# Loading the first weight piece in halves between the quarters of x, with the first squares taken bank by bank

## The chip, the core and the metric

The kernel runs on one core of a Trainium2 chip. The metric is the device time of one execution in microseconds; the number compared is the median of several runs. Five engines work side by side, each with its own queue in order: TensorE (PE, matrix products and transposes; its weight loads are PEld), VectorE (DVE), ScalarE (ACT), GpSimd (POOL) and SyncE (SP), which here only issues DMA transfers from HBM.

## What is computed

Two layers of an encoder on 256 tokens of width 1024, all in float32. What matters here is how the first layer begins:

```
def rms_norm(x, g, eps=1e-6):
    return x * rsqrt(mean(x * x, axis=-1) + eps) * g
def swiglu(x, w_in, w_out):
    gate, up = split(x @ w_in, 2, axis=-1)
    return (silu(gate) * up) @ w_out
for i in range(2):
    h = x + 0.5 * swiglu(rms_norm(x, norm_ffn1[i]), w_ffn1_in[i], w_ffn1_out[i])
    ...   # windowed attention beside a convolution, gated; a second swiglu; a gated input embedding
```

`w_ffn1_in` has 1024 rows and 2 x 2816 columns: 22 blocks of 128 gate columns and 22 of up columns.

## The kernel before, in words

**Products in three passes.** float32 operands are each split in a high and a low part (`w_hi`, `w_lo`, and `x0h`, `x0l` for the first x). A product is the sum of three: hi by hi, hi by the low part of x, low weight by hi. One block of 128 weight columns takes 8 row blocks (k = 0 to 7) times 3 matmuls, 24 in all. A gate block and an up block make a pair, `gate_up(j)`, with 48 matmuls and one PSUM tile `ps_gu`; there are 22 pairs. `by_pass` (line 349) runs the three passes one after the other over k, so that it can begin while `w_lo` is not there yet; `mm3` (line 338) goes through k once with three matmuls each and so needs both parts at once. Line 345 in the profile is mm3's matmul, line 354 by_pass's. Only pair 0 uses by_pass in the kernel before.

**Weights.** `Weights` (`ws`) keeps a list of units (one HBM transfer each into one of 5 `raw` buffers, line 83) and of specs (a 128-column piece, split by `prep_upto` into `w_hi` by a ScalarE cast, line 109, and `w_lo` by a VectorE subtraction, line 110; 7 buffers of each). `get()` hands out the next spec, first running hooks that are due, and then prepares specs up to 6 ahead; loading runs 3 units ahead of the unit that is being split. Specs 0 to 3 (pairs 0 and 1) have a unit of 512 KB each; after that a unit has 1 MB and serves two specs: units 4 and 5 serve specs 4 to 7 (pairs 2 and 3), units 6 and 7 the specs 8 to 11, and so on. The transfers go through SP's queue in order. x itself (`x_ld`, 1 MB, four transfers of a quarter, line 198) takes one of the 5 `raw` buffers too, so unit 4 can be loaded only when x has been transposed.

**The start.** PE first runs warm-up products (`work`, line 191; each shows as two records) on a constant, then transposes the parameter rows (`ps_par`, line 222) and x, 128 columns (one k) at a time with two transposes each (line 528), each k into a PSUM bank of its own; `WAIT[k]` puts extra `work` ahead of a k, and `BRIDGE` ahead of the first product. ScalarE makes `x0h` from PSUM with the norm's gain (line 534), VectorE `x0l` (line 535). Then spec 0 is split in two halves, and the first product begins. In between, x is copied to SBUF (`x32`, line 516), and its squares are formed: ScalarE squares one k (lines 446 and 448), GpSimd adds it to `sq_acc` (line 449). Here the order on ScalarE and VectorE is the program's (`manual_schedule`); later a scheduler with its own time model sets it, and `ws.behind` keeps the splits of later specs behind the last square.

**The norm.** The gate_up products use x without the norm's factor; it is multiplied in when `ps_gu` is read (`evac`, line 625). The factor comes from `Stat`: `divide` splits `sq_acc` into `sum_h` and `sum_l` (lines 503 and 504), `done` sums over the partitions by two matmuls (`ps_stat`, line 466), then come a square root on ScalarE (`sd`, line 414, with a table load) and a reciprocal on VectorE (line 416). `done` is due with spec 5. Until then no `ps_gu` can be read and freed. PSUM holds four one-bank tiles (`mm_tile`) and two two-bank tiles (`at_tile`); in the kernel before every `ps_gu` of the first stage is an `mm_tile`, and so is `ps_stat`.

**Late loads.** `hooks` call `late_loads` ahead of pair 1: 14 small transfers on SP's queue (line 562, parameters for later). `late_params` (hook ahead of pair 5) transposes the rows on PE (`ps_par`, line 222 again).

## Time and profile before

| what | value |
|---|---|
| runs | 1088.31, 1088.95 and 1089.26 us; median 1088.95 |
| profiled execution | 1086.72 us, of which the span of the program's instructions is 1084.9 |
| PE busy | 1076.1 us of the span |
| first product's first matmul | 9.65 us after the start |
| pair 1 begins | 15.32 us |
| pair 2 begins | 20.76 us |
| pair 3 begins | 29.54 us |
| last gate_up product ends | 133.65 us |

How to read it: times in a timeline count from the span's start. A PE instruction is listed with its whole duration (275 ns for a 128x256 matmul), but matmuls overlap and follow one another every 0.113 us, so the busy share of PE says only where it was not waiting. A note such as [0.83 <-DVE w_lo L110] says that the engine sat idle for 0.83 us until that instruction released it.

### The profile page before, as it was taken

The numbers are of one execution on the slowest core, as the hardware profiler recorded it, in microseconds if no ns is written. First come the engines' busy times: TensorE is split into PE (matmuls) and PEld (weight loads), VectorE is DVE, ScalarE is ACT, GpSimd is POOL, SyncE is SP. The second block draws the span as 40 slices with busy tenths as digits, with TensorE's granted clock in tenths as the row PEclk, the third lists the DMA queues.
The fourth block names the chain that finished last, engine by engine and source line by source line (L and its number), as shares of the span: only waits on it lengthen the run. The fifth ranks groups of instructions, "written<-read, shape, count | busy, mean of one in ns | idle before, by whom it ended". The sixth has DMA issues, their size and how long they took to land.

```text
span 1084.9 us, 22084 instructions
## 1 busy us (share of the span) xinstructions
PE 1076.1 (99%) x9180; PEld 1058.9 (98%) x9180; DVE 821.4 (76%) x1228; ACT 627.4 (58%) x1055; POOL 85.0 (8%) x156
## 2 busy tenths in 40 slices
PE   9999999999999999999999999999999999999998
PEld 8999999999899999999999999999998999999998
DVE  6777666799988777656887776669999987776664
ACT  7655445676766555445675554548776665554453
POOL 3100001120002000001110000112100100000110
PEclk9999999999999999999999999999999999999999
DMA  9786546556066656546555554666533666564531
GB/s 312 243 282 209 179 167 223 173 191 187 7 237 235 216 173 210 179 166 231 184 198 200 190 188 147 210 233 195 156 117 134 211 209 208 182 196 147 203 117 40
DMA packets 195612, 202.95 MB, mean 187 GB/s; under 512 B 3936, under 2 KB 188848, under 8 KB 195512
## 3 DMA queue, kind: packets, MB, share of 16 engines
q1 hardware_dynamic: 195480, 201.53, 56.0%
q8 instruction: 72, 1.18, 0.4%
q14 instruction: 28, 0.23, 0.1%
q10 hardware_dynamic: 32, 0.01, 0.0%
HBM read 200.46 MB, written 1.06 MB: 186 GB/s over the span
## 4 chain that ended last, share of the span: by engine, by line
PE 83%; DVE 9%; ACT 4%; issue 2%; POOL 1%; DMA 1%; SPq 0%; DVEq 0%; ACTq 0%; POOLq 0%
PE ps_gu L345 43%; PE ps_fo L345 22%; PE ps_wo L345 4%; DVE y L682 4%; PE ps_pe L345 4%; DVE w_lo L110 3%; PE ps_ao L959 3%; PE ps_c L345 2%; PE ps_co L1063 2%; ACT w_hi L109 1%; PE ps_pp L345 1%; DVE s L848 1%; PE ps_g L345 1%; ACT s L856 1%; DMA raw<-in_w_ffn_in_dram 1%
## 5 line engine op out<-in xcount | busy, mean ns | idle before, releaser
L110 DVE TENSOR_TENSOR w_lo<-raw,w_hi 128x1024 fp32r<-128x1024 f32 (+2 forms) x377 | 450.8, 1202 | 195.7 <-ACT w_hi L109 195.5
L109 ACT CAST w_hi<-raw 128x1024 fp32r<-128x1024 f32 (+2 forms) x377 | 387.7, 1034 | 352.1 <-PE ps_gu L345 189.7
L345 PE MATMUL ps_fo<-h_hi,w_hi 128*128 128x256 f32 x704 | 193.0, 275 | 0.0
L345 PE MATMUL ps_fo<-h_lo,w_hi 128*128 128x256 f32 x704 | 193.0, 275 | 0.0
L345 PE MATMUL ps_fo<-h_hi,w_lo 128*128 128x256 f32 x704 | 193.0, 275 | 0.0
L345 PEld LDWEIGHTS ps_fo<-h_hi,w_hi 128*128 128x128 f32 x704 | 131.9, 188 | 0.0
L345 PEld LDWEIGHTS ps_fo<-h_lo,w_hi 128*128 128x128 f32 x704 | 131.9, 188 | 0.0
L345 PEld LDWEIGHTS ps_fo<-h_hi,w_lo 128*128 128x128 f32 x704 | 131.9, 188 | 0.0
L449 POOL TENSOR_TENSOR sq_acc<-sq_acc,sq 128x256 f32<-128x256 f32 x56 | 52.9, 944 | 810.4 <-ACT sq L448 810.0
L682 DVE SCALAR_TENSOR_TENSOR y<-cpad,cw,y 128x256 f32<-128x256 f32 x240 | 100.7, 476 | 0.2
L345 PE MATMUL ps_gu<-xf0h,w_hi 128*128 128x256 f32 x352 | 96.8, 275 | 0.0
L345 PE MATMUL ps_gu<-xf1h,w_hi 128*128 128x256 f32 x352 | 96.8, 275 | 0.0
L345 PE MATMUL ps_gu<-xf0h,w_lo 128*128 128x256 f32 x352 | 96.7, 275 | 0.0
L345 PE MATMUL ps_gu<-xf1h,w_lo 128*128 128x256 f32 x352 | 96.7, 275 | 0.0
L345 PE MATMUL ps_gu<-xf0l,w_hi 128*128 128x256 f32 x352 | 96.7, 275 | 0.0
L345 PE MATMUL ps_gu<-xf1l,w_hi 128*128 128x256 f32 x352 | 96.7, 275 | 0.0
L345 PE MATMUL ps_gu<-xn0h,w_lo 128*128 128x256 f32 x352 | 96.6, 275 | 0.0
L345 PE MATMUL ps_gu<-xn0l,w_hi 128*128 128x256 f32 x352 | 96.6, 275 | 0.0
L345 PE MATMUL ps_gu<-xn0h,w_hi 128*128 128x256 f32 x352 | 96.5, 275 | 0.0
L345 PE MATMUL ps_gu<-x0h,w_hi 128*128 128x256 f32 x336 | 92.8, 276 | 1.7 <-ACT sd L414 1.7
L345 PE MATMUL ps_gu<-x0h,w_lo 128*128 128x256 f32 x336 | 92.6, 276 | 0.8 <-DVE w_lo L110 0.8
L345 PE MATMUL ps_gu<-x0l,w_hi 128*128 128x256 f32 x336 | 92.5, 275 | 0.0
(266 smaller groups left out, 2691.8 us busy)
## 6 DMA issues: line engine op xcount, KB each, us to landing
raw<-in_w_ffn_in_dram SPq DMA_DIRECT2D x86, 1024.0 KB
raw<-in_w_in_dram SPq DMA_DIRECT2D x30, 1024.0 KB
raw<-in_w_ffn_out_dram SPq DMA_DIRECT2D x32, 896.0 KB
raw<-in_w_ffn_out_dram SPq DMA_DIRECT2D x16, 1024.0 KB
raw<-in_w_o_dram SPq DMA_DIRECT2D x8, 1024.0 KB
raw<-in_w_pe_gate_dram SPq DMA_DIRECT2D x8, 1024.0 KB
raw<-in_w_attn_out_dram SPq DMA_DIRECT2D x8, 512.0 KB
raw<-in_w_conv_out_dram SPq DMA_DIRECT2D x4, 1024.0 KB
```

The costliest lines, as they stand in the source:

```text
L109: nc.scalar.copy(out=hv[:, at, d0 : d0 + w], in_=src),
L110: nc.vector.tensor_tensor(out=lv[:, at, d0 : d0 + w], in0=src, in1=hv[:, at, d0 : d0 + w].bitcast(F32), op=ALU.subtract,),
L345: mm = nc.tensor.matmul(ps, wa[:, k0 + k, cols], xa[:, kx, :], start=a, stop=b)
L449: nc.gpsimd.tensor_tensor(out=self.acc, in0=self.acc, in1=sq, op=ALU.add)
L682: last_tap[0] = nc.vector.scalar_tensor_tensor(out=y[:, i, :], in0=src, scalar=w, in1=y[:, i, :], op0=ALU.mult, op1=ALU.add)
L848: nc.vector.tensor_tensor_reduce(out=s[:, c, :], in0=ps[:, c, :], in1=bias[:, v * GROUP + c, off : off + T], scale=1.0, scalar=sink[:, hd ...
L856: nc.scalar.activation(out=s[:, c, :], in_=s[:, c, :], func=AF.Exp, bias=nm[:, c : c + 1], accum_out=den[:, c : c + 1],)
L959: nc.tensor.matmul(ps[:, c * T : (c + 1) * T], w[:, k, c * P : (c + 1) * P], x[:, k, :], start=k == 0, stop=k == KC - 1,)
L1063: mm = nc.tensor.matmul(ps[:, c, :], wa[:, k, c * P : (c + 1) * P], ya[:, k, :], start=(i, k) == (0, 0), stop=(i, k) == (2, KC - 1),)
```

## The change

Four things are changed, all in the first layer's start.

1. **Transfers.** Only two quarters of x are issued first. Unit 0 (and unit 1) are loaded as two halves of 4 k each, and the other two quarters of x are issued between and behind unit 0's halves: x0, x1, half a of unit 0, x2, half b, x3, unit 1 in halves, units 2 and 3.
2. **The first product.** PE transposes k = 0 to 3, does the hi-by-hi pass for them, transposes 4 and 5, does what has become possible, transposes 6 and 7, and does the rest. On ScalarE and VectorE the splits of x and of the weight's halves follow the same order. k and k + 4 share a PSUM bank. WARM goes from 7 to 6, WAIT from (0,0,1,0,2,0,2,0) to (0,0,2,0,0,0,0,0), BRIDGE from 4 to 2.
3. **Squares and copies.** Each bank (two k) is squared and copied to `x32` by one instruction of 512 columns. The first two squares go to a PSUM tile, the other two to SBUF; VectorE adds them, and GpSimd adds nothing. The splits of specs 2 to 5 are placed by hand between them, and `divide` runs in this order too, ahead of spec 5's split.
4. **Pairs.** Pairs 0, 1 and 2 go pass by pass, the others by mm3. Pair 0's `ps_gu` is an `at_tile`. `late_loads` moves from the hook ahead of pair 1 to that ahead of pair 2.

```
-WARM, WAIT, BRIDGE = 7, (0, 0, 1, 0, 2, 0, 2, 0), 4
+WARM, WAIT, BRIDGE = 6, (0, 0, 2, 0, 0, 0, 0, 0), 2
...
             for place, src in sources:
                 self.nc.sync.dma_start(place(v), src)
+                if self.next_load == 0:
+                    self.between.pop(0)()
...
+    ws.between = [lambda i=i: load_x(i) for i in (2, 3)]
...
-                        u = cols_unit(w_in, KD, c0 + c * P, P)
+                        u = cols_unit(w_in, KD, c0 + c * P, P, () if c else (KC,))
...
+    first_ps = at_tile("ps_gu").rearrange("p (c t) -> p c t", c=2)[:, :, :T]
...
+        splits = []
+        ws.cuts = (KC,)
+        ws.prep_upto(0, splits)
+        w_first = ws.ready[0]
+        turn_x(0, 1)
+        split_x(0, 1)
+        turn_x(2, 3)
+        split_x(2, 3)
+        work(BRIDGE, first_ps[:, 0, :])
+        for call in splits[:2]:
+            call()
+        steps((0, 0, 4))
+        turn_x(4, 5)
+        split_x(4, 5)
+        for call in splits[2:]:
+            call()
+        steps((1, 0, 4), (2, 0, 4), (0, 4, 6))
+        turn_x(6, 7)
+        split_x(6, 7)
+        steps((1, 4, 6), (2, 4, 6), (0, 6, 8), (1, 6, 8), (2, 6, 8))
         ws.prep_upto(1)
...
+        def keep_x(b):
+            nc.vector.tensor_copy(out=x32[:, b::KC, :], in_=banks[b])
+        ps_sq = at_tile("ps_sq").rearrange("p (b c t) -> p b c t", b=2, c=2)
+        sums = [tmp.tile([P, 2, T], F32, name="sq2", tag="gu") for _ in range(2)]
+        def square(b):
+            nc.scalar.activation(out=ps_sq[:, b] if b < 2 else sums[b - 2], in_=banks[b], func=AF.Square)
+        def plus(out, in0, in1):
+            nc.vector.tensor_tensor(out=out, in0=in0, in1=in1, op=ALU.add)
+        for b in range(2):
+            square(b)
+            keep_x(b)
+            ws.prep_upto(2 + b)
+        for b in range(2, KC):
+            square(b)
+            plus(sums[b - 2], sums[b - 2], ps_sq[:, b - 2])
+        plus(sums[0], sums[0], sums[1])
+        stat.acc = tmp.tile([P, T], F32, name="sq_acc", bufs=1)
+        plus(stat.acc, sums[0][:, 0, :], sums[0][:, 1, :])
+        ws.prep_upto(4)
+        divided, _ = stat.divide()
+        for b in range(2, KC):
+            keep_x(b)
+        ws.prep_upto(5)
+    ws.rest = LOOK
+    ws.get()
+    ws.rest = 0
+    ws.behind = (divided.ins,)
...
-            ps, products = pair("ps_gu", x_in, j == 0, early=x_in is x_first)
+            ps, products = pair("ps_gu", x_in, j == 0, early=x_in is x_first and j < 3)
...
-            hooks = {1: lambda: late_loads(hp), 5: late_params, 6: lambda: late_tables(hp), 8: late_write, 12: late_bias} if l == 0 else {}
+            hooks = {2: lambda: late_loads(hp), 5: late_params, 6: lambda: late_tables(hp), 8: late_write, 12: late_bias} if l == 0 else {}
```

`turn_x(k)` runs WAIT[k] and the two transposes of k, `split_x(k)` makes `x0h` and `x0l` of k, `splits` holds the cast and the subtraction of each half of spec 0, and `steps((pass, from, to), ...)` issues the matmuls of the first product for those k, pinned in this order on PE as every by_pass matmul now is.

## The prediction

> **What bounds the kernel now.** I read the page first, for the engine that is busy, then a table of stretches of the start, then the chain of waits through it.

> ```profile
> PE 1076.1 (99%) x9180; PEld 1058.9 (98%) x9180; DVE 821.4 (76%) x1228; ACT 627.4 (58%) x1055; POOL 85.0 (8%) x156
> ```
> ```profile
> 20.76:27.60 6.84, 6.01 (x52) 5.80 (x50) 6.84 (x7) 6.80 (x8) 0.11 (x1) 1.00 0.85 300
> 27.60:29.54 1.94, 0.21 (x2) 0.01 (x2) 1.94 (x3) 1.91 (x4) 0.00 (x0) 1.00 0.02 4
> 46.56:133.65 87.09, 87.09 (x771) 87.09 (x770) 64.34 (x88) 45.87 (x71) 0.00 (x0) 1.00 0.65 217
> ```

> PE (first busy column of the stretches) is the bound: it is idle for some 9 us of a span of 1084.9. So an edit is worth the idle PE time that it removes, and the rest of the kernel, which follows PE, moves along. In steady work 771 records take 87.09 us, 0.113 us a matmul, 2.72 for a block of 24 and 5.44 for a pair. The change touches nothing behind the first pairs, so only the start can pay: the first two stretches, in which PE stood for 0.83 and 1.73 us while DVE and ACT (third and fourth column) were full. The PE rows and the chain say on what:

> ```profile
> 4.62 1.11 PE L528 MATMUL ps_xt<-ident,x_ld 128*128 128x128 f32 x4
> 5.53 0.44 PE L191 MATMUL ps_xt<-ones_d 128*128 128x128 f32 x2
> 5.81 0.60 PE L528 MATMUL ps_xt<-ident,x_ld 128*128 128x128 f32 x4
> ```
> ```profile
> 9.65 1.26 PE L354 MATMUL ps_gu<-x0h,w_hi 128*128 128x256 f32 x8 [0.43 <-ACT w_hi L109]
> ...
> 15.32 0.28 PE L345 MATMUL ps_gu<-x0h,w_hi 128*128 128x256 f32 x1
> ...
> 22.00 0.39 PE L345 MATMUL ps_gu<-x0h,w_lo 128*128 128x256 f32 x1 [0.83 <-DVE w_lo L110]
> ...
> 29.54 0.39 PE L345 MATMUL ps_gu<-x0h,w_hi 128*128 128x256 f32 x1 [1.73 <-ACT sd L414]
> ```
> ```profile
> 15.97 1.62 POOL sq_acc L449
> ...
> 19.25 0.42 ACT sq L448
> 19.67 0.95 ACT w_hi L109
> ...
> 29.01 0.48 ACT sd L414
> ...
> 40.75 0.07 PE ps_par L222
> ```

> The squares pass to and fro between ACT and GpSimd until 19.67; only then comes spec 4's cast, too late for pair 2, which began at 20.76 and stood for 0.83 us until 22.00 for its `w_lo`. The same sum makes the root late: pair 3 waits until `sd` is done at 29.49, since four one-bank PSUM tiles hold pairs 0 to 2 and `ps_stat`.

> **The change part by part.** Prices come from these groups of the start on ACT and on DVE (busy time, then mean ns of one), the order from the ACT rows, the transfers from three stretches:

> ```profile
> L109 ACT CAST w_hi<-raw 128x1024 fp32r<-128x1024 f32 x3 | 3.2, 1053 | 0.4 <-DMA raw<-in_w_ffn_in_dram 0.4
> L448 ACT ACTIVATE sq<-x 128x256 f32<-128x256 f32 x3 | 1.1, 418 | 0.0
> L516 ACT COPY x<-ps_xt 128x256 f32<-128x256 f32 x2 | 0.6, 372 | 0.0
> L109 ACT CAST w_hi<-raw 128x512 fp32r<-128x512 f32 x1 | 0.6, 616 | 0.0
> ```
> ```profile
> L110 DVE TENSOR_TENSOR w_lo<-raw,w_hi 128x1024 fp32r<-128x1024 f32 x12 | 14.6, 1257 | 4.2 <-ACT w_hi L109 4.2
> L416 DVE RECIPROCAL r_x<-sd 128x256 f32<-128x256 f32 x1 | 1.7, 1740 | 0.0
> L516 DVE COPY x<-ps_xt 128x256 f32<-128x256 f32 x4 | 1.4, 416 | 0.0
> L110 DVE TENSOR_TENSOR w_lo<-raw,w_hi 128x512 fp32r<-128x512 f32 x2 | 1.3, 684 | 0.0
> L625 DVE TENSOR_TENSOR gu<-ps_gu,r_x 128x512 f32<-128x512 f32 x2 | 1.3, 673 | 0.0
> ```
> ```profile
> 5.42 3.42 ACT L534 ACTIVATE x0h<-ps_xt,par 128x256 fp32r<-128x256 f32 x8 [0.51 <-PE ps_xt L528]
> 8.98 1.14 ACT L109 CAST w_hi<-raw 128x512 fp32r<-128x512 f32 x2
> 10.51 1.06 ACT L109 CAST w_hi<-raw 128x1024 fp32r<-128x1024 f32 x1 [0.39 <-DMA raw<-in_w_ffn_in_dram]
> ```
> ```profile
> 1.80:4.00 2.20, 2.20 (x12) 2.20 (x12) 0.00 (x0) 0.69 (x1) 0.56 (x2) 1.00 0.86 261
> 4.00:6.50 2.50, 2.50 (x17) 2.24 (x16) 0.58 (x2) 1.26 (x4) 0.00 (x0) 1.00 0.79 245
> 6.50:10.50 4.00, 3.57 (x30) 3.26 (x29) 4.00 (x11) 3.39 (x8) 0.00 (x0) 1.00 1.14 343
> ```

> *Landings.* The last column is GB/s. x and two units are 2.10 MB; at these rates their data are through at 9.15, and ACT's cast of unit 1 waits for its transfer until 10.51 (the row with 0.39), so a landing comes 1.3 us behind its data. By the same rates the new order lands half a of unit 0 at 6.2, x2 at 7.2, half b at 8.2, x3 at 8.9, unit 1 at 10.5 as before. Two more DMA issues on SP (10 ahead of unit 4, where there were 8) cost nothing: unit 4 waits for x's buffer anyway.

> *First product.* PE is slow at first: four transposes take 1.11 at 4.62 and 0.60 at 5.81, some 0.21 apart against 0.11. A `work` is two such records, 0.42; with one fewer ahead, the first transposes come at 4.2 for 4.62, as x0 has landed by then (4.1 by the rates). One more `work` ahead of k = 2 keeps its transposes at 5.8. ACT makes one `x0h` in 0.42 (3.42 for 8), begins 0.8 after the transposes at first, 0.5 after them later: k = 0 to 3 are split at 7.1, cast a ends at 7.7, and the first matmul comes at 7.75 for 9.65. From there PE and ACT wait for each other by turns. Four matmuls and four transposes (0.11 each, 0.2 to restart) take PE to 8.7; k = 4 and 5 are split from 8.75 to 9.6, cast b ends at 10.1; the eight matmuls that PE has meanwhile end at 9.6, so it waits 0.5. Two matmuls and four transposes to 10.9; `x0h` of 6 and 7 from 11.0 to 11.8, `x0l` of 7 at 12.4 (0.5 behind), and the last three matmuls end at 12.8. Before, that was 15.32 - 2.72 = 12.6. The second product's casts (11.75 to 12.9) hide beside it; it ends at 15.5, where pair 1 stood at 15.32. So the earlier start gives nothing: **minus 0.2 us**. If ACT's part of the relay hid wholly, the first product would end at 11.4, 1.4 us better; with each of the three hand-overs 0.3 dearer, 0.9 worse.

> *Squares and copies.* The trace shows no square of 512 columns; bounds are 616 ns (the cast of that size) and twice 418. I take 640, near the cast, since the second halves of such instructions are cheaper. Copies of 512 lie between 673 (`gu`, also from PSUM) and twice 416, adds the same; I take 0.68, near `gu`. All must follow one another bank by bank. ACT: square 0 from 12.8, spec 2's cast to 14.4, square 1, spec 3's cast to 15.9, squares 2 and 3 to 17.0, spec 4's cast to 17.9, `sum_h` behind the last add. DVE: unit 1's halves to 13.7, copy 0, spec 2's `w_lo` to 15.7, copy 1, spec 3's to 17.4, four adds to 19.5, spec 4's to 20.6, `sum_l`, copies 2 and 3 to 22.1, spec 5's to 23.2, spec 6's to 24.3.

> *Pairs 1 and 2.* Pair 1 runs from 15.5 to 20.95. Going pass by pass, pair 2 needs spec 4's `w_hi` at 20.95 (there 3 us before) and its `w_lo` at 22.8 (2.2 before), spec 5's `w_lo` at 25.5 (2.3 before). With 0.23 for the two sum matmuls it ends at 26.6. At the dear ends above, ACT is 0.8 and DVE some 1 us later: still inside. The 0.83 stall goes.

> *Pair 3.* Pair 0 no longer holds a one-bank tile, so pair 3 takes the bank of x that copy 3 frees at 22.1 instead of waiting for `sd`; spec 6 is split by 24.3. What is late next is pair 4, at 32.1, which needs `sd` or an evacuation; the sum is split by 20.9 and its two matmuls come with spec 5, from 23.7, so `sd` is done by 26 or 27 (3 us allowed for casts ahead of it on ACT). The 1.73 stall goes.

> *Sum.* Pair 3 begins at 26.6 for 29.54 with 0.1 of restart: 3.0 us. I take off 0.1 for matmuls a little slower beside full engines: **2.9 us**.

> *The late loads moved.*

> ```profile
> 19.51 2.59 SPq L562 DMA_DIRECT2D rows_late<-in_norm_mix_dram  x1
> ...
> 27.72 0.55 SPq L562 DMA_DIRECT2D rows_late<-in_k_norm_dram  x2
> ```

> Ahead of them on SP now come units 9 and 10, which wait for the splits of specs 6 and 7 (24.3 and 25.5), so the rows' issues begin near 26. Before, ten of them took 8.8 us (19.51 to 28.27), behind weights in flight. So they are out by 35 and land by 36.3 (1.3 as above). Pair 5's hook, where PE transposes them, stood at 40.75 and comes at 37.5. Cover 1.2 us; if it is gone, PE waits, since it runs in order.

> The profiled execution took 1086.72, the median of the runs is 1088.95; I apply the difference to the median: 1088.95 - 2.9 = **1086.05**.

> **The rivals.** *Half the gain.* The hand-overs cost 0.9 more and pair 2 still waits, because ACT or DVE is later than I have it by 3 us (unit 4's landing would do that; it is issued only when k = 7 is transposed, near 11, for which the rates leave room). For it: DVE is at work without a break from 13 to 24. Gain 1.0: 1087.95.

> *PE at its first rate for longer.* The rows at 4.62 and 5.81 show the change of rate; the granted clock (the column ahead of the DMA share) reads 1.00 in every stretch, so only the spacing tells. With one `work` less and pauses in PE's queue the switch could come one step later, behind k = 3 and the relay's start: twelve records more at 0.1 each, and two tails of 0.15, 1.5 us lost, gain 1.4: 1087.55. [...]

> *The relay hides.* First product ends at 11.4: gain 4.3, 1084.65.

> *Slower: the rows come too late.* If SP's order puts units 11 and 12 ahead of the late loads (their buffers are free only when specs 8 to 11 are split, near 30), the rows' issues run from 31 to 40 and later, and land at 41 to 43. PE then stands at pair 5's hook from 37.5, with all products behind it. It turns the change to a loss when they land after 40.4 (37.5 + 2.9), and to over 0.2% when after 42.6; at 43 it is 5.5 - 2.9 = 2.6 slower, 1091.55. Against it: the hook stands ahead of those loads in the program, and before the change the issues did begin as soon as unit 8 was out.

> **How the numbers follow.** 0.2% is 2.2 us, about what a measurement can tell from no change. Forecast 0.57; half the gain 0.16; first rate longer 0.10; relay hides 0.09; rows too late 0.08. Faster by over 0.2% means under 1086.77: the forecast but for 0.05 of it, the hidden relay, and 0.02 of the clock's: 0.63. Slower: 0.08. Same: 0.29. The range reaches from the hidden relay to just past half the gain, 1084.6 to 1088.3, and leaves out the late rows and small tails.

> **What would show it.** In the profile after: first L354-type matmul near 7.75 and pair 1 near 15.5, no earlier; no GpSimd adds before 30 us; no PE wait over 0.3 us between 13 and 32; pair 3 near 26.6; `ps_par` near 37.5 with no wait; PE busy the same 1076 or so. Wrong, if PE waits for `w_lo` or `sd` again, if transposes stand 0.21 apart past 6 us, or if PE waits at `ps_par`.

## The result and the profile after

The kernel after takes 1083.8 us (median of 6 runs, 1082.99 to 1084.65), the kernel before 1089.33 (6 runs, 1088.31 to 1089.93): a ratio of 0.995, with a 95% interval of 0.9937 to 0.9962. That is 5.5 us for the 2.9 that I forecast, and below my range. The profiled execution of after took 1084.65, with a span of 1082.9; that of before had 1086.72 and 1084.9. So the two profiles lie 2.1 us apart and the two medians 5.5, and this is the riddle of the case. One run of the kernel before on the second chip below (1349.58 us at a clock of 0.752, a slow state) is left out of all counts.

The page's first line for the kernel after, and its stretches over the same times as those shown of before (after the length: busy time of PE, PEld, DVE, ACT, POOL, the granted clock, the DMA share, GB/s):

```profile
PE 1075.6 (99%) x9168; PEld 1058.3 (98%) x9168; DVE 823.0 (76%) x1231; ACT 625.5 (58%) x1050; POOL 78.8 (7%) x149
```
```profile
20.76:27.60 6.84, 6.84 (x63) 6.84 (x62) 6.84 (x9) 6.81 (x8) 0.00 (x0) 1.00 1.09 380
27.60:29.54 1.94, 1.94 (x20) 1.94 (x19) 1.94 (x2) 1.94 (x3) 0.00 (x0) 1.00 1.05 356
43.90:130.96 87.06, 87.06 (x770) 87.06 (x769) 63.63 (x88) 46.69 (x73) 0.81 (x6) 1.00 0.70 236
```

PE is now full in both stretches in which it had stood, with DVE and ACT as full as before. The steady stretch has its old length, 87.06 for 87.09; it begins and ends 2.7 us earlier (130.96 for 133.65). PE's rows, then ACT's and DVE's:

```profile
5.96 1.06 PE L540 MATMUL ps_xt<-ident,x_ld 128*128 128x128 f32 x4
...
8.09 0.74 PE L371 MATMUL ps_gu<-x0h,w_hi 128*128 128x256 f32 x4 [0.48 <-ACT w_hi L112]
...
10.48 0.51 PE L371 MATMUL ps_gu<-x0h,w_hi 128*128 128x256 f32 x2 [0.27 <-ACT w_hi L112]
...
13.14 1.11 PE L371 MATMUL ps_gu<-x0h,w_hi 128*128 128x256 f32 x8
...
15.90 1.07 PE L371 MATMUL ps_gu<-x0h,w_hi 128*128 128x256 f32 x8
...
21.34 1.07 PE L371 MATMUL ps_gu<-x0h,w_hi 128*128 128x256 f32 x8
...
26.34 1.07 PE L371 MATMUL ps_gu<-x0h,w_lo 128*128 128x256 f32 x8
27.25 0.28 PE L358 MATMUL ps_gu<-x0h,w_hi 128*128 128x256 f32 x1
```
```profile
9.09 0.84 ACT L549 ACTIVATE x0h<-ps_xt,par 128x256 fp32r<-128x256 f32 x2 [1.05 <-PE ps_xt L540]
...
11.25 0.84 ACT L549 ACTIVATE x0h<-ps_xt,par 128x256 fp32r<-128x256 f32 x2 [0.81 <-PE ps_xt L540]
...
13.01 0.59 ACT L588 ACTIVATE ps_sq<-ps_xt 128x512 f32<-128x512 f32 x1
...
25.93 0.48 ACT L432 ACTIVATE sd<-ps_stat,eps 128x256 f32<-128x256 f32 x1
```
```profile
13.84 0.68 DVE L581 COPY x<-ps_xt 128x512 f32<-128x512 f32 x1
...
19.85 1.22 DVE L113 TENSOR_TENSOR w_lo<-raw,w_hi 128x1024 fp32r<-128x1024 f32 x1
20.99 0.42 DVE L523 TENSOR_TENSOR sum_l<-sq_acc,sum_h 128x256 fp32r<-128x256 f32 x1
```

The first product ends at 13.14, pairs 1 and 2 begin at 15.90 and 21.34, pair 3 goes on from 27.25 behind pair 2's last pass (two of its matmuls had slipped in at 26.11), and the root is done at 26.41 instead of 29.49. The start is the one that I worked out, some 0.35 us late. One of my signs of being wrong is there too: the four transposes at 5.96 still stand 0.2 us apart, since PE came to its full rate only at 7.20, not at 5.65 as in before's profile. That belongs to the 0.35 us and makes the gain smaller, not larger. So what is missing is not in these two profiles.

### The profile page after: what moved, and what is told of

Read it like the earlier page. It is cut to its first block, busy times and chain, and to the rows that moved or that the text cites. A ratio compares the mean times of both kernels' runs of the same rounds, so it can differ in the third digit from the quotient of the medians.

```text
span 1082.9 us, 22050 instructions
## 1 busy us (share of the span) xinstructions
PE 1075.6 (99%) x9168; PEld 1058.3 (98%) x9168; DVE 823.0 (76%) x1231; ACT 625.5 (58%) x1050; POOL 78.8 (7%) x149
## 3 DMA queue, kind: packets, MB, share of 16 engines
HBM read 200.46 MB, written 1.06 MB: 186 GB/s over the span
## 4 chain that ended last, share of the span: by engine, by line
PE 90%; DVE 5%; ACT 3%; issue 1%; POOL 0%; ACTq 0%; DVEq 0%; POOLq 0%
PE ps_gu L358 43%; PE ps_fo L358 22%; PE ps_wo L358 4%; PE ps_pe L358 4%; PE ps_c L358 3%; PE ps_g L358 3%; PE ps_ao L1019 3%; DVE y L742 3%; PE ps_co L1123 2%; DVE w_lo L113 2%; PE ps_gu L371 2%; PE ps_pp L358 1%; ACT s L916 1%; ACT w_hi L112 1%; ACT s L927 1%
## 5 line engine op out<-in xcount | busy, mean ns | idle before, releaser
L467 POOL TENSOR_TENSOR sq_acc<-sq_acc,sq 128x256 f32<-128x256 f32 x49 | 46.0, 940 | 788.1 <-ACT sq L466 788.1
L358 PE MATMUL ps_gu<-x0h,w_hi 128*128 128x256 f32 x304 | 83.8, 276 | 0.0
L358 PE MATMUL ps_gu<-x0l,w_hi 128*128 128x256 f32 x304 | 83.6, 275 | 0.0
L358 PE MATMUL ps_gu<-x0h,w_lo 128*128 128x256 f32 x304 | 83.5, 275 | 0.0
```

Source lines behind the costliest of these rows:

```text
L358: mm = nc.tensor.matmul(ps, wa[:, k0 + k, cols], xa[:, kx, :], start=a, stop=b)
L467: nc.gpsimd.tensor_tensor(out=self.acc, in0=self.acc, in1=sq, op=ALU.add)
```

## The experiments

Twelve experiments, in three batches; each batch had its own chip and its own runs of the kernel before. In the first batch theory P put the extra gain down to the start: fewer dummy products, which run while PE is still at its first, slow rate (records 0.21 us apart for 0.11). Theory S, its rival, had it that the two waits alone make the difference, and that before's profiled execution was fast for a reason elsewhere.

**The two kernels again** (no edit).

> The kernel before, unchanged. Its profiled execution took 1086.72 us and PE came to its full rate at 5.65 us; its timed runs took 1088.31 to 1089.93. Theory P (the rate change falls at another time in each execution, and PE's extra work at the start is paid at the slow rate): this profile shows the change later than 5.7 us, the first product later than 9.65 by about half of the shift, and a total 1 to 3 us above 1086.72. Theory S (the stalls alone make the difference between the two kernels, and the profiled execution was fast for a reason elsewhere): the first product again near 9.65, pair 3 near 29.5, and the surplus lies behind 30 us.

> The changed kernel, unchanged. Its profile had the full rate from 7.2 us and took 1084.65, the longest of its six runs (1082.99 to 1084.65). Theory P: with an earlier change of rate the first matmul comes before 8.09 by up to 0.9 us and the total falls to about 1083; with a later one it stays near 1084.7. Theory S: the start is the same, and the spread lies elsewhere.

Before: 1088.46 (11 runs), beside 1089.39 for the 21 shared runs of it. After: 1084.61 (5 runs), ratio 0.9952 (0.9939 to 0.9964). After's second profile has the times of my forecast within 0.06 us (first matmul 7.69, product's end 12.75, pair 1 at 15.51):

```profile
7.69 0.74 PE L371 MATMUL ps_gu<-x0h,w_hi 128*128 128x256 f32 x4 [0.77 <-ACT w_hi L112]
...
12.75 1.11 PE L371 MATMUL ps_gu<-x0h,w_hi 128*128 128x256 f32 x8
...
15.51 1.07 PE L371 MATMUL ps_gu<-x0h,w_hi 128*128 128x256 f32 x8
```

In before's second profile the first product began at 10.01 for 9.65, since a quarter of x came later, and pair 3 at 30.18 for 29.54:

```profile
30.18 0.38 PE L345 MATMUL ps_gu<-x0h,w_hi 128*128 128x256 f32 x1 [1.95 <-ACT sd L414]
```

That is not theory P's way: PE came to its full rate earlier than in the first profile (4.51 for 5.65), and the product began later. The span is 1.46 us longer (1086.38 for 1084.92): 0.64 of it is there when pair 3 begins, and 0.8 comes behind the first attention stage. The profile that I had predicted from was a favourable one.

**The dummy products exchanged.**

```
 before: WARM, WAIT, BRIDGE = 6, (0, 0, 2, 0, 0, 0, 0, 0), 2
 after:  WARM, WAIT, BRIDGE = 7, (0, 0, 1, 0, 2, 0, 2, 0), 4
```

> The kernel before with the changed kernel's warm-up counts alone: 6, 2 ahead of k = 2, 2 ahead of the first product, none else (21 records of 128 columns become 14 plus none between the later transposes; 16 of 32 are left). Theory P: it is 1 to 2.5 us faster than before, about 1087. Theory S: within 0.5 us of before, since the casts and squares behind it set pairs 2 and 3.

> The changed kernel with the counts of before: 7 at the start, 1, 2 and 2 ahead of k = 2, 4 and 6, and 4 ahead of the first product. Theory P: 0.5 to 1.5 us slower than the changed kernel, about 1085, since the later ones now stand in the relay. Theory S: within 0.5 us of it.

Before with after's counts: 1089.67, ratio 0.9997 (0.9988 to 1.0006). After with before's: 1085.28, ratio 0.9959 (0.9946 to 0.9971). The first of the two rules theory P out as the source of the missing gain: P had some 1087 for it. The second is less clear. It is 0.7 above after's 1084.61, which P had said (0.5 to 1.5) and theory S not quite (within 0.5), but the five runs of each overlap. Its profile has full rate from 4.25 us and ends the first product at 13.13, where profiles of after's counts with full rate from 4.48 and 4.55 have 12.12 and 12.15; so dummy products in the relay may cost something. But the profile of the first one held what the first profile of before had not. Its stretches:

```profile
26.77:30.18 3.41, 1.19 (x11) 0.98 (x9) 3.41 (x4) 3.38 (x5) 0.00 (x0) 1.00 0.07 20
30.18:33.59 3.41, 3.37 (x16) 3.38 (x17) 3.41 (x4) 0.92 (x1) 0.83 (x5) 0.50 0.49 105
33.59:40.00 6.41, 6.41 (x58) 6.41 (x58) 1.12 (x3) 1.51 (x2) 3.31 (x27) 1.00 1.01 348
```

Read the column of the granted clock: 1.00, then 0.50 for 3.41 us, then 1.00. PE had waited for the root until 30.22, and the stretch behind the wait went at half rate: 16 matmuls in 3.41 us, where a full-rate stretch has some 30. That is 1.7 us which my sum lacked. Every run lists its mean clock, and 3.41 us at half rate take 0.0016 from it. Of before's 32 unchanged runs in this batch, 22 have a mean clock of 0.998 or less (median 1089.6) and 10 have 0.999 or 1.000 (1088.14); all runs of after have 0.999 or 1.000. From here on theory R: the wait ahead of pair 3 costs its own length and, in many executions, a stretch at half rate behind it. Its rival is theory L: its length alone.

**Theory R tried on the kernel before: the wait kept, PE kept busy in it.**

```
+            if x_in is x_first and j == 3:
+                work(8, at_tile("ps_fill"))
             ps, products = pair("ps_gu", x_in, j == 0, early=x_in is x_first)
```

> The kernel before, with eight dummy 128x128 products put on PE between pair 2 and pair 3, into a PSUM tile that nothing else needs: they fill some 1.8 us of PE's wait for the square root, and take nothing from the wait itself. They leave every other instruction as it is. Theory R (the wait at pair 3 leaves PE idle for so long that the clock is halved for one stretch of 3.41 us just behind it, in some 70 of 100 executions): the mean granted clock of all runs is 0.999 to 1.000, none 0.998, pair 3 still begins near 30, and the median falls by 0.7 x 1.7 = 1.2 us, to about 1088.2. Theory L (the wait costs only its own length, and the rest of the gain comes from elsewhere): no change, 1089.4, ratio 1.000. A third way, slower by up to 0.3 us, if the dummy products end behind the root.

```profile
27.03 1.95 PE L191 MATMUL ps_fill<-ones_d 128*128 128x128 f32 x16
29.81 0.39 PE L345 MATMUL ps_gu<-x0h,w_hi 128*128 128x256 f32 x1 [0.83 <-ACT sd L414]
```

Pair 3 begins no earlier than in before's first profile (29.81 for 29.54), and yet the median is 1087.23 (11 runs) for 1088.26, ratio 0.999 (0.9981 to 0.9999). All 11 runs have a clock of 0.999 or 1.000, where 12 of before's 26 on this chip have less. Before's own runs of full clock have 1087.32 there. Useless products bring 1.0 us, as R says; under theory L they could bring none.

**Theory R tried on the kernel after: the wait put back.** A dummy product ahead of pair 3 reads the sum after six, or eight, more adds on GpSimd; the dummy goes into the bank that pair 3 overwrites.

```
             ps, products = pair("ps_gu", x_in, j == 0, early=x_in is x_first and j < 3)
+            if x_in is x_first and j == 3:
+                held = stat_in.acc
+                for _ in range(6):          # 8 in the long one
+                    nc.gpsimd.tensor_tensor(out=held, in0=held, in1=held, op=ALU.add)
+                tc.keep_in_program_order(nc.tensor.matmul(ps[:, 0, :P], ones_d, held[:, :P], start=True, stop=True))
```

> The kernel after, with a wait put back on PE ahead of pair 3: one dummy 128x128 product that reads the sum of squares after six more adds on GpSimd (0.75 to 1.1 us each in the kernel before, from about 21.5 when the sum has been split). By these PE stands from about 26.9 until 27.0 to 28.2: a wait of 0.1 to 1.3 us. Theory R: a wait that short costs its own length and no more, 1084.7 to 1085.9, and the mean clock stays at 0.999 to 1.000. Theory L: the same. It is the control for the longer wait.

> The same with eight adds: PE stands from about 26.9 until 29 to 30.4, a wait of 2 to 3.5 us, as long as the one of the kernel before or longer. Theory R: most runs show a mean clock of 0.998 and cost the wait plus 1.7 us: 1084.6 + 2.7 + 1.7 = about 1089; those with a clock of 1.000 cost the wait alone; the record of the granted clock reads 0.50 for 3.41 us behind the wait. Theory L: the wait alone, about 1087.3, and a clock of 1.000 in all runs.

The waits were 2.17 and 3.27 us. The second lies in the range that I gave (2 to 3.5); the first is longer than I had sized it (0.1 to 1.3), since its six adds took 7.52 us, 1.25 each, and PE came to the place at 26.15 for the 26.9 that I took. So the first is no control, but a copy of before's wait. Its row and its stretches, and then the stretches of the long one:

```profile
28.32 0.78 PE L686 MATMUL ps_gu<-sq_acc,ones_d 128*128 128x128 f32 x2 [2.17 <-POOL sq_acc L685]
```
```profile
24.96:28.37 3.41, 1.24 (x12) 1.04 (x10) 3.41 (x3) 3.40 (x5) 3.15 (x3) 1.00 1.06 366
28.37:31.78 3.41, 3.41 (x16) 3.41 (x17) 3.41 (x4) 1.81 (x2) 0.00 (x0) 0.50 1.02 349
```
```profile
26.59:30.00 3.41, 0.34 (x4) 0.14 (x2) 3.41 (x4) 3.25 (x4) 3.17 (x4) 1.00 1.01 343
30.00:33.42 3.42, 3.21 (x15) 3.21 (x16) 3.42 (x3) 0.00 (x0) 0.15 (x1) 0.50 0.86 283
```

With 2.17 us: median 1087.27 (11 runs), in two kinds: 3 runs of full clock at 1085.93, and 8 of 0.998 at 1087.71. Against 1083.69 for the next kernel on this chip, which has no wait, that is 2.2 us, the wait, and 4.0, the wait and 1.8 more. With 3.27 us: 1089.19 (11 runs), every run at 0.998 or less. R has 1083.69 + 3.27 + 1.7 = 1088.7 for this wait; the rest may be a second such stretch, since three of the runs have a clock of 0.996, but none of these was profiled. R holds in both directions, and theory L, which had 1087.3 for the long wait, doesn't.

**One part undone: no relay.** x's quarters first, unit 0 whole, all transposes ahead of the first product, before's dummy products; the squares and pairs of after stay.

```
-    for i in range(2):
+    for i in range(4):
         load_x(i)
...
+        for k in range(KD):
+            turn_x(k)
+            split_x(k)
+        for call in splits:
+            call()
+        work(BRIDGE, first_ps[:, 0, :])
+        steps(*ALL)
```

> The kernel after without its first part: x's four quarters loaded one behind the other, then unit 0 in one transfer, all transposes ahead of the first product, and the dummy products of the kernel before; the squares per bank, the copies, the pass-by-pass pairs and the late loads are those of the kernel after. My prediction's step (the halves between the quarters give nothing): the first product ends at 12.4 to 13.0, pair 3 begins at 26.5 to 27.0, the time is that of the kernel after, 1084.6 +- 0.4. The rival (the relay makes part of the gain, since it makes the start less open to a late transfer of x): the first product ends at 13 to 13.5, time 1085.0 to 1085.6. In both the clock stays at 0.999 to 1.000.

```profile
10.07 1.26 PE L371 MATMUL ps_gu<-x0h,w_hi 128*128 128x256 f32 x8 [0.32 <-ACT w_hi L112]
...
13.02 1.07 PE L371 MATMUL ps_gu<-x0h,w_hi 128*128 128x256 f32 x8
```

The first product starts two us later and ends at 13.02, within after's 12.75 to 13.21; the time is 1083.69 (5 runs), ratio 0.9954 (0.9941 to 0.9967). The halves between the quarters bring nothing that these medians show (after has 1083.77 to 1084.61 on the other chips; it was not run on this one), as my step said. The gain lies in the rest of the change.

**Three edits of the kernel after, beside it.**

> The kernel after, unchanged, for the other three of this batch to be compared with on one chip. All theories: 1083.7 to 1085.0, mean clock 0.999 to 1.000 in every run, the products' times of the earlier runs (first product ends 12.7 to 13.2, pair 3 begins 26.6 to 27.1).

The control: 1083.77 (5 runs), ratio 0.9965 (0.9951 to 0.9978); on this chip 4 of before's 10 runs have a clock of 0.998, and before's median is lower, 1087.82.

The old squares: `keep_x(k)` and `stat.add(x32[:, k, :])` of the kernel before in place of the squares per bank, and `stat.finish(5, ahead=1)`.

> The kernel after with the squares of the kernel before: x copied k by k, eight squares of 256 columns on ACT, added one by one on GpSimd, the sum split later. The relay, the pass-by-pass pairs, the late loads, and the place of the first pair's sums (a two-bank tile, so that pair 3 finds a free bank) stay. Theory R with 'the bank counts': the root is late again (29 or so for 26.5), but pair 3 no longer needs it, since x's bank is free from about 18; only spec 4's late cast costs, up to 0.8 us in pair 2: 1084.7 to 1085.4, clock 0.999 to 1.000. Rival ('the sum counts'): without the early sum PE stands 1.5 to 2.5 us ahead of pair 3 or 4, with some runs at a clock of 0.998: 1086.3 to 1088.

```profile
29.02 0.58 PE L485 MATMUL ps_stat<-sum_h,ones_r 128*128 128x256 f32 x1 [3.95 <-ACT sum_h L522]
```
```profile
24.40:27.81 3.41, 0.67 (x6) 0.47 (x5) 3.41 (x3) 2.11 (x4) 2.34 (x2) 1.00 1.09 385
27.81:31.22 3.41, 2.20 (x10) 2.20 (x11) 3.41 (x4) 1.16 (x2) 0.00 (x0) 0.50 1.04 346
31.22:34.64 3.42, 3.42 (x18) 3.42 (x18) 0.42 (x2) 0.09 (x1) 0.00 (x0) 0.50 0.42 143
```

1091.73 (5 runs), 8.0 slower than the control, and slower than before (ratio 1.0042, 1.003 to 1.0055). Both of my expectations missed: PE waits neither for a bank nor at pair 3, but 3.95 us at the sum's own matmul, which stands ahead of pair 2's second product in its order; and two stretches of half rate follow, in which PE was busy for 2.20 and 3.42 us, so 2.8 us are lost. With 0.7 us ahead of pair 1 (16.59, where 13.14 and one block of 2.72 would give 15.9) this makes 7.5, as much as lies between the profiled executions of the two (1091.60 and 1084.13); the medians are 8.0 apart. So the early sum is needed where the sum's matmul stands; whether the free bank alone would do, with that matmul moved back, this kernel could not tell, and it stays open.

PE's order in the relay: transposes of k = 4 and 5 ahead of the first matmul, those of 6 and 7 behind the second pass.

```
-        steps((0, 0, 4))
         turn_x(4, 5)
         split_x(4, 5)
+        steps((0, 0, 4), (1, 0, 4))
         for call in splits[2:]:
             call()
-        steps((1, 0, 4), (2, 0, 4), (0, 4, 6))
         turn_x(6, 7)
         split_x(6, 7)
-        steps((1, 4, 6), (2, 4, 6), (0, 6, 8), (1, 6, 8), (2, 6, 8))
+        steps((2, 0, 4), (0, 4, 6), (1, 4, 6), (2, 4, 6), (0, 6, 8), (1, 6, 8), (2, 6, 8))
```

> The kernel after with PE's order in the first product changed: the transposes of k = 4 and 5 stand ahead of the product's first matmul, those of 6 and 7 behind its second pass over k = 0 to 3, with ACT's and VectorE's order as it is. In the kernel after ACT waits 1.05 us for the transposes of 4 and 5 and 0.8 us for those of 6 and 7. If these waits set the relay: ACT has x0h of 4 and 5 at 8.4 to 8.5, cast b at 9.1, x0h of 6 and 7 at 10.1 to 10.3, and the first product ends at 11.1 to 11.5, 1.3 to 1.7 us sooner, all behind it too: 1083.0 to 1083.4 where the kernel after has 1084.6. Rival: x's third and fourth quarter land too late for it (6.6 and 8.4 at the earliest), or pairs 1 and 2 then wait for casts or weights: gain under 0.4 us.

```profile
7.41 0.61 ACT L112 CAST w_hi<-raw 128x512 fp32r<-128x512 f32 x1
7.92 0.84 ACT L549 ACTIVATE x0h<-ps_xt,par 128x256 fp32r<-128x256 f32 x2
8.64 0.62 ACT L112 CAST w_hi<-raw 128x512 fp32r<-128x512 f32 x1
9.54 0.84 ACT L549 ACTIVATE x0h<-ps_xt,par 128x256 fp32r<-128x256 f32 x2 [0.27 <-PE ps_xt L540]
```
```profile
8.07 0.74 PE L371 MATMUL ps_gu<-x0h,w_hi 128*128 128x256 f32 x4 [0.19 <-ACT w_hi L112]
...
11.44 1.11 PE L371 MATMUL ps_gu<-x0h,w_hi 128*128 128x256 f32 x8
```

ACT's waits of 1.05 and 0.81 us are down to none and 0.27, the first product ends at 11.44 (control: 13.21), and all behind it follows. 1082.17 (5 runs, 1081.51 to 1083.37), 1.6 us under the control (1082.70 to 1084.63); ratio to before 0.9952 (0.994 to 0.9965). The two ranges overlap, with five runs each, but the shift of 1.8 us in PE's rows is as large as the gain. This version has the lowest median of all kernels here.

Pairs 1 and 2 in the ordinary order.

```
-            ps, products = pair("ps_gu", x_in, j == 0, early=x_in is x_first and j < 3)
+            ps, products = pair("ps_gu", x_in, j == 0, early=x_in is x_first and j < 1)
```

> The kernel after with pairs 1 and 2 in the ordinary order again (three matmuls for each k, so the first needs w_hi and w_lo at once). My prediction's step has w_lo of spec 4 at 20.6 and pair 2 at 20.95, of spec 5 at 23.2 for 23.7: no wait or one of 0.2 us, the time that of the control +- 0.2. Rival: the pass-by-pass order is what takes the 0.83 us wait away, and PE stands 0.5 to 1 us in pair 2 again: control + 0.5 to + 1.0, clock still 1.000.

```profile
20.35:26.03 5.68, 5.68 (x53) 5.68 (x51) 5.68 (x7) 4.17 (x5) 0.00 (x0) 1.00 1.08 384
```

PE has no gap in pair 2. 1084.3 (6 runs, 1083.12 to 1086.94) against the control's 1083.77, with overlapping runs: no difference that these runs can show. (Its profiled execution is 1.0 us shorter than the control's, and its first product ended 1.1 us earlier; the last section says why.) The early `w_lo` takes the 0.83 us wait away, not the order of the passes.

## Why the prediction was wrong

Step by step, most of it held. *First product*: 12.8 forecast, and 12.12 to 13.21 in the seven profiles that begin as after does, 12.77 on the mean; without the relay it is 13.02 in one profile, with a like median on another chip, so "the earlier start gives nothing" is borne out as far as these runs tell. My waits were mis-sized in detail (0.5 forecast, 0.27 found for cast b), with no effect on the sum. *Squares and copies*: 590 ns for a square of 512 columns (I took 640) and 0.68 us for a copy (as taken); the sum was split by 21.4 for 20.9. *Pairs 1 and 2*, *pair 3*: both waits went, and pair 3 began at 26.63 to 27.07 for my 26.6. *Late loads*: the rows' last issue ended at 36.2 and PE's transposes of them at 38.07 waited for nothing. The sum "2.9 us" is 2.69 between the two profiles that I was given, at the end of the first gate_up stage. Of the rivals, none came true as a time. *PE at its first rate for longer* did show in after's profile, but for some 0.35 us and not the 1.5 at which I priced it. The relay did not hide; the time at which I priced that, 1084.65, came near the result by another way.

The step that failed is the last: "The profiled execution took 1086.72, the median of the runs is 1088.95; I apply the difference to the median". The profile lay 2.2 us below the median, below every run shown. I noted that and passed on, as if those 2.2 us had nothing to do with what the change removes. They did, in two ways.

- *The price of the 1.73 us wait lacks the stretch at half rate behind it.* By their mean clocks it is in 38 of the 68 unchanged runs of before over the three chips (22 of 32, 12 of 26, 4 of 10), in none of the 37 runs of the versions of after that have no wait, and not in the profile that I read. The runs with it are 1.4 to 1.9 us longer (1089.6 for 1088.14, 1089.23 for 1087.32, 1088.58 for 1087.19). Dummy products in the wait remove it, a wait put back brings it back.
- *The wait and the start were short in that profile.* Pair 3 began at 29.54 there, at 30.18 and 30.22 in the two other profiles of before or with its counts changed, against 26.63 to 27.07 in after's three: 3.1 on the mean of each. These three of after have late starts (first product's end 13.03 on the mean, for 12.77 over seven), so 3.3 is nearer. Between the two medians of full clock on the first chip (1088.14 and 1084.61) it is 3.5, where I had 2.9.

Together: 3.5 + 1.5 x 22/32 = 4.5 us, where the means on the first chip differ by 4.75 (1089.23 and 1084.47) and the medians by 4.8, since more than half of before's runs have the stretch. The first measurement's 5.5 is 0.7 more than that, with six runs each; what made it so much is not settled.

## What to carry to other kernels

When the profiled execution is faster than every timed run, ask first what the slower runs contain, and whether the change touches it; the list of mean clocks answers this before any profile does. A wait of PE is to be priced at its length plus what the clock does behind it, here up to twice its length (4.0 us for a wait of 2.17). And where two engines hand work to each other in turns, put the producer's next input ahead of the consumer's ready work: moving four transposes ahead of four matmuls that could already run gave 1.6 us that the relay itself hadn't.

## What the runs showed of the hardware

**The clock changed at edges 3.41 us apart that don't start with the kernel's work.** PE's first record begins at 1.12 us in the first profiles of both kernels, and the trace's record of the granted clock has full rate begin at 5.65 in one and at 7.20 in the other. In every profile with a half-rate stretch its edges lie a whole number of 3.413 us behind that point: 30.18 is 6.29 + 7 x 3.413 in the kernel before with fewer dummy products, 28.37 is 4.48 + 7 x 3.413 with the shorter wait, 30.00 is 6.11 + 7 x 3.413 with the longer, 27.81 is 7.33 + 6 x 3.413 with the old squares. So the same wait can lie within one stretch or across an edge. The stretches of the two profiles of before that kept full rate, cut at the same grid (first the original, then the repeat):

```profile
26.13:29.54 3.41, 1.68 (x15) 1.48 (x14) 3.41 (x4) 3.38 (x5) 0.00 (x0) 1.00 0.06 17
29.54:32.95 3.41, 3.41 (x29) 3.41 (x30) 3.41 (x4) 0.89 (x1) 0.97 (x1) 1.00 0.49 82
```
```profile
24.99:28.40 3.41, 3.24 (x28) 3.04 (x27) 3.41 (x5) 3.10 (x5) 0.00 (x0) 1.00 0.61 210
28.40:31.81 3.41, 1.63 (x14) 1.63 (x15) 3.41 (x3) 2.65 (x3) 0.00 (x0) 1.00 0.19 39
```

**The same phase moves the start.** In the kernels that begin as after does, the first product ended at 12.12 with full rate from 4.48, at 12.15 from 4.55, at 12.75 from 5.76, at 12.91 from 6.11, and at 13.14 to 13.21 from 7.08 to 7.33. The row for 4.55 (pairs 1 and 2 in the ordinary order), to be held against after's 13.14:

```profile
12.15 1.10 PE L371 MATMUL ps_gu<-x0h,w_hi 128*128 128x256 f32 x8
```

So up to 1.1 us between two profiles of kernels with the same start (13.21 for 12.12) can come from the point at which full rate begins, and a small edit of the start is to be judged beside a profile of like phase.

**The first attention stage has two lengths.** From the first `ps_kv` matmul to the first `ps_ao` matmul it took 91.24 us in before's profile and 92.04 in after's, and both values come up in either kernel (92.02 in before with fewer dummy products, 91.24 in after with more). This hides 0.8 us of the gain between the two profiles that I was given. The rest of the kernel, from the first `ps_ao` matmul to the end, has two lengths as well: 795.3 to 795.5 us in most profiles, 796.1 to 796.3 in three of the four on the first chip. What chooses these values was not looked into.
